# A hybrid decoder block: Toeplitz transfers issued by POOL, and two groups of loads kept in program order

## The chip, the cores and the metric

The kernel runs on one core of one Trainium2 chip. A core has five engines, each with its own queue of instructions that it works off in order: PE (TensorE, matmuls), DVE (VectorE), ACT (ScalarE), POOL (GpSimd) and SP (SyncE, which here only issues DMA transfers). A transfer is issued by an engine's queue and then moved by 16 DMA engines that all queues share. Transfers issued by SP appear in the profile under the hardware queue, those issued by POOL under the software queue. The metric is the device time of one execution, in microseconds (us); lower is better. The time before is the median of three runs, 1581.86 us (1578.76 to 1582.31).

## The reference

One decoder block over 1024 tokens and 16 meta tokens, model width 1024, float32. Two mixers run on one projection of the layer-normed input, their gated sum is projected and added, and a feed-forward layer follows:

```
p     = h @ w_in + b_in          # u_s5 | q | k | v | o | i | f | g_s5 | g_m
y_s5  = z[..., :D] * sigmoid(z[..., D:]),  z = gelu(S5(u_s5)) @ s5_w_glu
y_m   = (sigmoid(o) * HeadNorm(mLSTM(silu(conv(q,k)), v, i, f))) @ m_w_out
mix   = sigmoid(g_s5) * y_s5 + sigmoid(g_m) * y_m
h     = LN(alpha * h + mix @ w_o)
h     = LN(alpha * h + relu(h @ w_up + b_up)^2 @ w_down)
```

S5 is a linear state-space recurrence: 32 groups of 16 channels, each with 64 complex states, `x_t = Abar x_{t-1} + Bbar u_t`, `y_t = Re(C x_t) + D u_t`.

## The kernel before

Activations are kept with the feature on the partition. Each float32 product is made of three matmuls in a reduced format (lines 226 to 228): both operands are split into a high and a low part (`whi`, `wlo` for weights; `hT_hi`, `hT_lo` for activations), with ACT copying the high part and DVE subtracting it for the low one. Weights come in as `wraw`, by line 198 for plain jobs and by line 1024 for the stage described below.

The projection runs as a list of jobs (q, k, v, o, u, g for each tile of columns), and smaller work is woven between the jobs' matmuls: lanes of generators are advanced as estimated PE time passes, each `yield` naming how long to wait until the next piece. The S5 mixer, the mLSTM's chunks and the preparation of later weights are such lanes. The order that is written this way is only a draft: a scheduler (line 2074) reorders the instructions of every engine by its own estimate of durations, within the data dependencies. Instructions wrapped in `tc.keep_in_program_order` keep the order in which they were written among themselves.

**S5.** The 32 groups go through in four blocks b = 0 to 3 of eight groups. The 1024 + 16 positions are cut into 130 columns of 8 steps. `s5_consts(b)` makes the matrices of a block: `s5Mi` (input to state), `s5RS` (state to output), `s5Kt` (the convolution kernel of the 8 steps, 32 partitions) and from it `s5Mx`, the lower-triangular Toeplitz matrix. POOL clears `s5Mx` (line 753), and sixteen small transfers (line 758: 8 shifts x 2 halves, 16 partitions x 4 x 128 down to 16 elements, 32 KB down to 4 KB) lay `s5Kt` out along its diagonals; 64 of them in all. Then POOL writes the first two columns of the rotation table `s5T` (lines 764 to 767), and DVE doubles it seven times (lines 572 to 577).

`u_load(b)` brings the block's input back from memory, regrouped, as `s5U` in eight transfers (line 786). `s5_batch(b)` multiplies it into states on PE (`s5z`, line 802; ACT and DVE move the result out, lines 810 and 812), scans them on DVE (lines 817 to 846, tables `s5T`, result `s5w`) and makes the output on PE (`s5y`: line 857 with `s5Mx` and `s5U`, line 858 with `s5RS` and `s5w`). It is stored to `ys_dr` (line 863), read back regrouped in eight transfers `s5yc` (line 871), and after the GELU split into `gelh` and `gell` (lines 877 and 878) for the GLU jobs z0 to z7.

**Then** come the GLU jobs, and a stage called `Seven`, a seven-product scheme in place of eight for the last gates (`g`) and for `m_w_out` (`y`). It needs sums of weights, which POOL makes by accumulating transfers during the projection (`ws_dr`, line 974, each behind a small copy `mark`, line 972, that waits for a job's weights), activations as `rawb` (line 991, eight transfers of 512 KB) with sums on DVE (line 1002) and splits (lines 997 and 998), and its weights by line 1024 into a ring of three buffers, split at lines 1042 and 1043.

**Beside it** run two lanes whose transfers share SP's queue: `ah_scale` (loads `ahr` 1377, DVE 1386, stores `ah_dr` 1388) and `up_early` (loads `wur` 1404, sums on DVE, stores `wu_dr` 1414), which prepares weight sums for the feed-forward layer. The tiles named here live in one pool of 30 slots of 4 KB per partition, so a load can also wait until the last reader of its slot is done.

Of the kernel before, what the change touches and what calls it, by code (L numbers as in the profile page):

```python
# [14 lines left out]
P = 128  # L15
# [97 lines left out]
def decoder_block(  # L113
# [4 lines left out]
    nc = tc.nc  # L118
    v_, a_, g_, t_ = nc.vector, nc.scalar, nc.gpsimd, nc.tensor
# [9 lines left out]
    def slot(name, dt=F32):  # L129
        return big.tile([P, SLOT], dt, tag="s", name=name)  # L130
# [404 lines left out]
    def u_job(i):  # L535
        st = {}

        def evac(bi, c0, c1, ps):
            if bi == 0:
                st["u"] = slot("uT")  # L540
            o = st["u"][:, :LEN].rearrange("p (j c) -> p c j", j=8)
            a_.activation(o[:, c0 // 8:c1 // 8, :], ps.rearrange("p (c j) -> p c j", j=8), AF.Identity,
                          bias=bft[:, JU + i:JU + i + 1])

        def done():
            nc.sync.dma_start(us_dr[i * P:(i + 1) * P].rearrange("p j c -> p (j c)"), st["u"][:, :LEN])
            UD.add(i)
            lanes["s5c"].add(s5_consts(i))
            lanes["s5"].add(s5_batch(i))
        fm_job(JU + i, BLK, 0, evac, done)  # L550
# [123 lines left out]
    def s5_consts(b):  # L674
# [49 lines left out]
        for ri in range(2):  # L724
            for g2 in range(2):
                s = slice(64 * g2, 64 * g2 + 64)
# [27 lines left out]
        mx = Mx[:, 0:1024].rearrange("p (q g t) -> p q g t", q=4, g=2)  # L754
        kt = Kt.rearrange("p (q t) -> p q t", q=4)
        for j in range(8):
            for g2 in range(2):
                nc.sync.dma_start(mx[16 * j:16 * j + 16, :, g2, 16 * j:P],
                                  kt[16 * g2:16 * g2 + 16, :, 0:P - 16 * j])
        yield K5[b]  # L760
        T = slot("s5T")
        tc_, ts_ = (T[:, i * 520:(i + 1) * 520].rearrange("p (q c) -> p q c", q=4) for i in range(2))
# [220 lines left out]
    def s3(t):  # L983
        return t[:, :1024].rearrange("p (k s) -> p k s", k=2)

    def raw_block(dr, kh, ch, off=0):
        ts = [slot("rawb"), slot("rawb")]
        for i in range(2):
            k = 4 * kh + 2 * i
            c = off + 512 * ch  # L990
            nc.sync.dma_start(s3(ts[i]), dr[k:k + 2, :, c:c + 512].rearrange("k p s -> p k s"))
        return ts

    def to_home(ts, hm):
# [9 lines left out]
    class Seven:  # L1004
# [8 lines left out]
        def load(self, i):  # L1013
            if i >= self.ntile():
                return
            r = ring[0].tile([P, 1024], F32, tag="wr", bufs=3, name="wraw")
            for j, (n, p) in enumerate(self.units[2 * i:2 * i + 2]):
                s = {5: 0, 6: 1, 7: 2, 3: 3}.get(n)
                if s is None:
                    t = self.w[self.i0 + 2 * p + (n == 4)].rearrange("p k f -> p (k f)")  # L1020
                    a = t[:, 0:512] if n == 1 else t[:, 512:1024]
                else:
                    a = ws_dr[self.p0 + p, s]
                nc.sync.dma_start(r[:, j * 512:j * 512 + 512], a)
            self.raw[i] = r

        def split(self, i):
# [115 lines left out]
    def gates_and_output():  # L1143
# [5 lines left out]
        def begin():  # L1149
            for nm, kh, ch in (("12", 0, 1), ("22", 1, 1), ("11", 0, 0), ("21", 1, 0)):  # L1150
                R[nm] = raw_block(h_dr, kh, ch, META)
# [12 lines left out]
        def hm_load():  # L1164
            for nm, kh, ch in (("11", 0, 0), ("12", 0, 1), ("22", 1, 1), ("21", 1, 0)):
                M[nm] = raw_block(hm_dr, kh, ch)
# [250 lines left out]
    for w in ORDER.split():  # L1417
        n, i = w[0], int(w[1:])
# [22 lines left out]
    for w in LOAD0.split():  # L1441
        i = int(w[1])
# [635 lines left out]
```

## Time and profile before

| what | value |
| --- | --- |
| runs | 1581.86 us median (1578.76 to 1582.31) |
| profiled execution | 1577.87 us, span from first to last instruction 1576.1 us |
| mean granted TensorE clock | 0.984 |
| PE busy | 1516.2 us, 96% |
| DVE, ACT, POOL busy | 1079.4, 642.8 and 70.2 us (68, 41 and 4%) |
| line 758 on SP | 64 transfers, median 593 ns each |
| hardware queue, software queue | 234.18 MB and 25.82 MB |

A busy share is an average over the whole span; a stage is read from a table of stages. In a row of a timeline stand the start, the duration, engine, line, operation, output and input, a count (xN: as many in a row), and in brackets the idle time just before with what ended it. A row of waits reads: engine, tile and line that waited, what it waited for, total us, number of times, longest. An engine with a q (SPq) stands for its queue, where issuing and waiting for a transfer is shown. In rows of a line's transfers the three durations are minimum, median and maximum in ns.

### The profile page before, as it was taken

The page shows a single profiled execution, that of the slowest core. Times are in us where ns is not written, and L with a number is a line of the kernel's source. Part 1 is how long each engine was busy: PE and PEld are TensorE (multiplying, and loading weights), DVE is VectorE, ACT ScalarE, POOL GpSimd, SP SyncE. Part 2 cuts the span into 40 slices and gives each one's busy share as a digit, 9 for nine tenths or more (in the row PEclk, how much of TensorE's full clock was granted, in tenths as well). Part 3 has the DMA queues.
Part 4 walks back from the last instruction along what each step waited for, and adds up shares of the span by engine and source line. Part 5 has one row for each costly group of instructions (what it writes and reads, how often), then busy time and mean ns, then how long its engine had stood idle before and what let it go on. Part 6 is the DMA issues. An engine that isn't in the chain of part 4 may idle for free.

```text
span 1576.1 us, 20513 instructions
## 1 busy us (share of the span) xinstructions
PE 1516.2 (96%) x7593; PEld 1278.9 (81%) x7593; DVE 1079.4 (68%) x2083; ACT 642.8 (41%) x982; POOL 70.2 (4%) x131
## 2 busy tenths in 40 slices
PE   8999999998899798999999999999999999999997
PEld 8998998997777686777788888888888888888886
DVE  7666555678667455568879575666666779776776
ACT  6523444335254333235635234444444534433340
POOL 0000011111001010000000001000000000000000
PEclk9999999999999899999999999999999999999999
DMA  8412324414344466685344317744443799667642
GB/s 310 157 56 63 97 61 133 119 31 121 108 115 99 151 181 217 226 317 200 102 149 144 108 54 242 246 145 149 147 147 134 220 366 335 220 227 239 222 166 107
DMA packets 140580, 261.31 MB, mean 166 GB/s; under 512 B 34224, under 2 KB 56184, under 8 KB 140424
## 3 DMA queue, kind: packets, MB, share of 16 engines
q1 hardware_dynamic: 116464, 234.18, 43.8%
q0 software_dynamic: 24016, 25.82, 6.7%
q8 instruction: 59, 0.97, 0.2%
q14 instruction: 41, 0.34, 0.1%
HBM read 188.78 MB, written 84.55 MB: 173 GB/s over the span
## 4 chain that ended last, share of the span: by engine, by line
PE 39%; issue 15%; DMA 2%; DVE 1%; ACT 0%; SPq 0%; POOLq 0%; DVEq 0%; ACTq 0%
PE mm L228 10%; PE mm L227 9%; PE mm L226 9%; PE sd L227 3%; PE sd L226 3%; PE sd L228 3%; DMA wur<-in_wup_dram 1%; DMA wu_dr<-wpre 1%; DMA rawb<-h_dr 1%; PE ln L1565 0%; DVE rawb L1002 0%; DVE wpre L1413 0%; DVE sgs L945 0%; DVE z2s L944 0%; DVE wlo L1043 0%
## 5 line engine op out<-in xcount | busy, mean ns | idle before, releaser
L226 PE MATMUL mm<-hT_hi,whi 128*128 128x512 f32 (+3 forms) x604 | 229.0, 379 | 1.4 <-ACT whi L212 1.4
L228 PE MATMUL mm<-hT_hi,wlo 128*128 128x512 f32 (+3 forms) x604 | 224.7, 377 | 3.9 <-DVE wlo L1043 3.9
L227 PE MATMUL mm<-hT_lo,whi 128*128 128x512 f32 (+3 forms) x604 | 227.5, 377 | 0.0
L228 PEld LDWEIGHTS mm<-hT_hi,wlo 128*128 128x128 f32 x604 | 113.7, 188 | 22.5 <-DVE wlo L1043 5.2
L226 PEld LDWEIGHTS mm<-hT_hi,whi 128*128 128x128 f32 x604 | 114.2, 189 | 19.6 <-ACT whi L212 1.8
L227 PEld LDWEIGHTS mm<-hT_lo,whi 128*128 128x128 f32 x604 | 114.1, 189 | 17.7 <-issue 0.4
L227 PE MATMUL sd<-dwl,dah 128*128 128x512 f32 x240 | 94.4, 393 | 0.0
L228 PE MATMUL sd<-dwh,dal 128*128 128x512 f32 x240 | 94.1, 393 | 0.0
L1777 ACT ACTIVATE dwh<-wdr 128x1024 fp32r<-128x1024 f32 x56 | 59.0, 1054 | 86.2 <-DMA wdr<-in_wdn_dram 28.1
L226 PE MATMUL sd<-dwh,dah 128*128 128x512 f32 x240 | 94.1, 393 | 0.0
L1773 ACT ACTIVATE dah<-da 128x1024 fp32r<-128x1024 f32 x56 | 58.7, 1051 | 84.8 <-PE sd L227 37.8
L1774 DVE TENSOR_TENSOR dal<-da,dah 128x1024 fp32r<-128x1024 f32 x56 | 68.2, 1220 | 24.1 <-ACT dah L1773 23.5
L227 PE MATMUL mm<-dwl,dah 128*128 128x512 f32 (+1 forms) x224 | 84.5, 378 | 0.0
L228 PE MATMUL mm<-dwh,dal 128*128 128x512 f32 (+1 forms) x224 | 84.4, 377 | 0.0
L226 PE MATMUL mm<-dwh,dah 128*128 128x512 f32 (+1 forms) x224 | 84.2, 377 | 0.0
L1778 DVE TENSOR_TENSOR dwl<-wdr,dwh 128x1024 fp32r<-128x1024 f32 x56 | 68.2, 1220 | 12.4 <-ACT dwh L1777 11.8
L226 PE MATMUL mm<-whi,hT_hi 128*128 128x256 f32 (+1 forms) x256 | 75.3, 294 | 0.0
L228 PE MATMUL mm<-whi,hT_lo 128*128 128x256 f32 (+1 forms) x256 | 74.6, 291 | 0.0
L227 PE MATMUL mm<-wlo,hT_hi 128*128 128x256 f32 (+1 forms) x256 | 73.9, 289 | 0.0
L213 DVE TENSOR_TENSOR wlo<-wraw,whi 128x1024 fp32r<-128x1024 f32 (+1 forms) x46 | 56.1, 1223 | 18.0 <-ACT whi L212 15.2
L228 PE MATMUL mm<-th,wul 128*128 128x512 f32 x156 | 61.6, 395 | 0.0
L227 PE MATMUL mm<-tl,wuh 128*128 128x512 f32 x156 | 61.5, 394 | 0.0
(473 smaller groups left out, 3679.8 us busy)
## 6 DMA issues: line engine op xcount, KB each, us to landing
da<-act_dr SPq DMA_DIRECT2D x56, 512.0 KB, 5.5
wdr<-in_wdn_dram SPq DMA_DIRECT2D x56, 512.0 KB, 6.2
wur<-in_wup_dram SPq DMA_DIRECT2D x32, 512.0 KB, 4.4
act_dr<-upy SPq DMA_DIRECT2D x64, 256.0 KB, 2.5
wraw<-in_wf_dram SPq DMA_DIRECT2D x30, 512.0 KB, 6.7
wu_dr<-wpre SPq DMA_DIRECT2D x21, 512.0 KB, 4.5
wpre<-wu_dr POOLq DMA_DIRECT2D x21, 512.0 KB, 5.3
act_dr<-upx SPq DMA_DIRECT2D x32, 256.0 KB, 3.0
```

Source lines behind the costliest of these rows:

```text
L213: todo.append(lambda e=v_, r=r, hi=hi, lo=lo, n=n: e.tensor_tensor(lo[:, :n], r[:, :n], f32(hi[:, :n]), op=OP.subtract))
L226: t_.matmul(ps, ah, bh, start=(i == 0 and part[0]), stop=False, skip_group_check=skip)
L227: t_.matmul(ps, ah, bl, start=False, stop=False, skip_group_check=skip)
L228: t_.matmul(ps, al, bh, start=False, stop=(i == n - 1 and part[1]), skip_group_check=skip)
L1773: a_.activation(ah[:, :D], a[:, :D], AF.Copy)
L1774: v_.tensor_tensor(alo[:, :D], a[:, :D], f32(ah[:, :D]), op=OP.subtract)
L1777: a_.activation(wh, raw[i], AF.Copy)
L1778: v_.tensor_tensor(wl, raw[i], f32(wh), op=OP.subtract)
```

## The change

Three edits. The sixteen transfers of each `s5Mx` go from SP's queue to POOL's. The loads of `rawb` (line 991) and the weight loads of `Seven` (line 1024) are wrapped so that they keep the order in which the program writes them.

```diff
@@ s5_consts
-                nc.sync.dma_start(mx[16 * j:16 * j + 16, :, g2, 16 * j:P],
-                                  kt[16 * g2:16 * g2 + 16, :, 0:P - 16 * j])
+                g_.dma_start(mx[16 * j:16 * j + 16, :, g2, 16 * j:P],
+                              kt[16 * g2:16 * g2 + 16, :, 0:P - 16 * j])
@@ raw_block
-            nc.sync.dma_start(s3(ts[i]), dr[k:k + 2, :, c:c + 512].rearrange("k p s -> p k s"))
+            tc.keep_in_program_order(nc.sync.dma_start(s3(ts[i]), dr[k:k + 2, :, c:c + 512].rearrange("k p s -> p k s")))
@@ Seven.load
-                nc.sync.dma_start(r[:, j * 512:j * 512 + 512], a)
+                tc.keep_in_program_order(nc.sync.dma_start(r[:, j * 512:j * 512 + 512], a))
```

Since the scheduler orders each engine, the three edits move instructions elsewhere too; the differences run from the constants of block 0 to the output projection. On SP, at the loads of block 1's input, this is the difference (minus: the row stood here before; plus: it stands here now; x7: seven in a row; the last numbers are the shape):

```order
-L786 DMA s5U<-us_dr 16x8x130 x7
-L758 DMA s5Mx<-s5Kt 16x4x128 x2
...
-L758 DMA s5Mx<-s5Kt 16x4x16 x2
-L786 DMA s5U<-us_dr 16x8x130
+L546 DMA us_dr<-uT 128x1040
+L198 DMA wraw<-in_wf_dram 128x1024
+L786 DMA s5U<-us_dr 16x8x130 x8
 L198 DMA wraw<-in_wf_dram 128x1024
```

The sixteen Toeplitz transfers that stood between the seventh and the eighth load are gone, and the eight loads stand together. The same holds for block 3, where three loads stood ahead of the transfers and five behind them. On POOL, at block 0, the transfers are put ahead of the first columns of the rotation table:

```order
 L753 MEMSET s5Mx 128x1024
+L758 DMA s5Mx<-s5Kt 16x4x128 x2
+L758 DMA s5Mx<-s5Kt 16x4x112 x2
+L758 DMA s5Mx<-s5Kt 16x4x96 x2
+L758 DMA s5Mx<-s5Kt 16x4x80 x2
+L758 DMA s5Mx<-s5Kt 16x4x64 x2
+L758 DMA s5Mx<-s5Kt 16x4x48 x2
+L758 DMA s5Mx<-s5Kt 16x4x32 x2
+L758 DMA s5Mx<-s5Kt 16x4x16 x2
 L764 MEMSET s5T 128x4
```

In blocks 1 to 3 they stand behind these columns (lines 764 to 767) and ahead of the next `mark` and `ws_dr`. The third place is on SP ahead of the gate products of `Seven`; the six loads of `in_wf` are those of its first three weight tiles:

```order
 L1372 DMA bB_5618<-in_ln0r_dram 128x1024
 L1377 DMA ahr<-ah_dr 128x1024
-L1024 DMA wraw<-in_wf_dram 128x512 x6
 L1388 DMA ah_dr<-ahr 128x1024
...
 L991 DMA rawb<-h_dr 128x2x512 x8
+L1024 DMA wraw<-in_wf_dram 128x512 x6
 L1024 DMA wraw<-ws_dr 128x512 x6
```

They stood behind the first load of `ah_scale` and now stand behind the eight `rawb` loads. On DVE the low part of the first of these tiles (line 1043) moves behind the first three sums of line 1002 and the next ones, to where the second tile's stood; on ACT its high part (line 1042) moves behind the first `hT_hi` of line 997. On PE the `s5z` matmuls of blocks 1 and 3 are spread over more places, and block 0's `s5y` with `s5w` (line 858) stands some 36 matmuls later.

## The prediction

> **What bounds the kernel now.** I read the page's engine shares first, then the stage table, then what PE (TensorE) waits for, then the timelines round the waits that the change can touch.
>
> ```profile
> PE 1516.2 (96%) x7593; PEld 1278.9 (81%) x7593; DVE 1079.4 (68%) x2083; ACT 642.8 (41%) x982; POOL 70.2 (4%) x131
> ...
> 360.00:400.00 40.00, 28.70 (x167) 26.03 (x166) 28.99 (x91) 18.28 (x27) 7.09 (x7) 0.85 0.42 120
> ...
> 520.00:560.00 40.00, 30.44 (x133) 24.98 (x132) 20.07 (x53) 8.46 (x16) 3.00 (x3) 0.87 0.49 149
> ...
> 720.00:1576.00 856.00, 847.12 (x3734) 689.33 (x3732) 614.83 (x897) 353.62 (x529) 12.36 (x22) 1.00 0.55 186
> ```
>
> The first row says that PE bounds the kernel: 1516.2 of a 1576.1 us span, so 60 us of idle time are all that reordering can win. The stage rows (length, then busy us of PE, PEld, DVE, ACT, POOL, the granted clock, DMA share, GB/s) say where they lie: 11.3 us between 360 and 400 and 9.6 us between 520 and 560, with a granted clock of 0.85 and 0.87 in just these stages. Behind 720 PE idles 9 us in 856, and there the change reorders only a few loads.
>
> ```profile
> PE s5z L802 <- DMA s5U<-us_dr: 15.3, 2, 9.6
> PE mm L227 <- DVE gell L878: 7.0, 1, 7.0
> PE s5y L858 <- DVE s5w L846: 6.0, 3, 4.3
> PE mm L228 <- DVE wlo L1043: 3.9, 2, 2.8
> ```
>
> These are PE's four largest waits (total us, times, longest). All four lie inside the region that the change reorders; the first is the loads of S5 input that stand on SP's queue among the Toeplitz transfers:
>
> ```profile
> 368.62 6.73 SPq L786 DMA_DIRECT2D s5U<-us_dr  x7
> 378.24 11.42 SPq L758 DMA_DIRECT2D s5Mx<-s5Kt  x16
> 389.70 0.58 SPq L786 DMA_DIRECT2D s5U<-us_dr  x1
> ...
> 500.68 1.27 SPq L786 DMA_DIRECT2D s5U<-us_dr  x3
> 514.88 10.82 SPq L758 DMA_DIRECT2D s5Mx<-s5Kt  x16
> 532.71 2.20 SPq L786 DMA_DIRECT2D s5U<-us_dr  x5
> ```
>
> Seven of block 1's eight pieces go out by 375.4; the eighth stands behind sixteen Mx transfers and leaves at 389.70. In block 3 five of eight stand behind them and leave at 532.71. PE answers:
>
> ```profile
> 398.38 2.07 PE L802 MATMUL s5z<-s5U,s5Mi 128*128 128x130 f32 x8 [5.73 <-DMA s5U<-us_dr]
> ...
> 400.32 0.78 PE L226 MATMUL mm<-hT_hi,whi 128*128 128x512 f32 x1
> ...
> 401.64 0.39 PE L227 MATMUL mm<-hT_lo,whi 128*128 128x512 f32 x1
> 401.87 0.40 PE L228 MATMUL mm<-hT_hi,wlo 128*128 128x512 f32 x1
> ...
> 537.46 2.94 PE L802 MATMUL s5z<-s5U,s5Mi 128*128 128x130 f32 x12 [9.56 <-DMA s5U<-us_dr]
> ```
>
> **The change, part by part.**
>
> *The eighth and the last five pieces leave early.* With the Mx transfers on POOL, the eight loads stand together on SP. Block 1's eighth would leave by about 375.8; even at the slowest landing of that line (8.7 us, the next fence) it is there at 384.5, and PE stood idle only from 392.65. That removes 5.73 us and the slow restart behind it: three steps from 400.32 to 401.64 took 1.32 us where the steady pace (401.64 to 401.87) makes it 0.69, so 0.6 us more. **A = -6.4 us.** In block 3 the five leave with the first three near 501–504 and are there by about 512, against an idle PE from 527.9: 9.56 + 0.6, **B = -10.2 us.** Both rest on no other wait taking the place.
>
> ```profile
> DMA to landing us min/median/max: 2.3/3.8/8.7
> ...
> L758 SPq DMA_DIRECT2D s5Mx<-s5Kt x64: 585/593/1835, 329.5 to 525.1; - x64
> ...
> L1621 POOL DMA_DIRECT2D wpre<-wu_dr x21: 527/528/616, 834.4 to 992.0; - x21
> ...
> L974 POOL DMA_DIRECT2D ws_dr<-in_wmo_dram x6: 1117/1354/1942, 267.8 to 620.3; - x6
> ...
> L766 POOL COPY s5T<-s_p x4: 189/480/5255, 325.1 to 502.8; 128x4 f32<-128x4 f32 x4
> ```
>
> *What POOL pays.* No Mx transfer was ever issued on POOL, so its price is bounded: below by POOL's loads of 128x1024 (0.53 us), above by its largest weight sum (1.94 us). An Mx piece is small and plain, so I take 0.6 us: 16 x 0.6 = 9.6 us for a block, 38 us in all on an engine that is busy for 4%. For blocks 1 to 3 the issues stand behind the block's T copies and ahead of the next ws_dr sum; what waits is the s5y matmul. Block 3's last piece went out at 525.7 on SP, and the first matmul that reads it stood at 557.9 (about 539 with A to C): 12 us to spare at least, and block 0, the one without spare time, is next.
>
> ```profile
> L857 PE MATMUL s5y<-s5U,s5Mx x16: 271/275/275, 557.9 to 573.7; 128*128 128x128 f32 x16
> ...
> 329.45 10.89 SPq L758 DMA_DIRECT2D s5Mx<-s5Kt  x16
> ...
> 325.01 0.10 POOL L764 MEMSET s5T<- 128x4 f32 x1 [11.39 <-PE s5p L733]
> ...
> 331.25 0.16 DVE L572 TENSOR_TENSOR s5tt<-s5T 128x4 f32<-128x4 f32 x1
> ...
> 349.24 0.15 DVE L577 TENSOR_TENSOR s5T<-s5tt 128x4 f32<-128x4 f32 x1
> ...
> 359.84 0.70 DVE L817 TENSOR_TENSOR s5w<-s5Z,s5T 128x520 f32<-128x520 f32 x1
> ```
>
> *Block 0.* POOL's T start (325.01) now stands behind the sixteen issues, which can begin only at 329.45: 329.45 + 9.6 = 339, and the DVE doublings, which took 331.25 to 349.4 mixed with other work, end at 357 if they take the same 18 us. Their reader L817 stood at 359.84, so the cover is 3 us. PE's L858 that waited 4.3 us here is now placed about 36 matmuls (36 x 0.23 = 8.3 us) later. So the stall becomes 4.3 - 8.3 + d for a chain late by d: gone at d = 0 (-4.3), +8 at d = 16. I take **C = -2 us.**
>
> ```profile
> 546.09 0.38 SPq L1377 DMA_DIRECT2D ahr<-ah_dr  x1
> 558.47 3.56 SPq L1024 DMA_DIRECT2D wraw<-in_wf_dram  x6
> ...
> 580.72 0.38 SPq L863 DMA_DIRECT2D ys_dr<-s5Y  x1
> ...
> 616.30 0.79 PE L227 MATMUL mm<-gell,whi 128*128 128x512 f32 x1 [7.04 <-DVE gell L878]
> ```
>
> *The six weight loads of L1024 leave this place.* They held SP from 546.5 to 562.0, and the ahr loads, the last ys_dr store and its reads stood behind them; PE's wait for the last gell at 616.30 ends that chain. It can lose all 7.0 us or nothing, as ahr work still precedes gell on DVE: **D = -4 us.**
>
> *Where they go.* They now stand behind the eight rawb loads, and the first whi/wlo of the gate run go where the second tile's stood:
>
> ```profile
> 694.10 5.93 SPq L991 DMA_DIRECT2D rawb<-h_dr  x8
> ...
> 707.42 1.22 DVE L1043 TENSOR_TENSOR wlo<-wraw,whi 128x1024 fp32r<-128x1024 f32 x1
> ...
> 716.04 1.22 DVE L1043 TENSOR_TENSOR wlo<-wraw,whi 128x1024 fp32r<-128x1024 f32 x1
> ...
> 717.31 0.50 PE L228 MATMUL mm<-hT_hi,wlo 128*128 128x512 f32 x1 [2.79 <-DVE wlo L1043]
> ```
>
> Tile 0 is then ready at 717.3, not 708.6; PE has 24 matmuls of it to do (24 x 0.23 = 5.6 us) before it reaches the second tile, where it stood at 717.31 before. That is +5.6; +10 if the loads also land late (last issue at 700.0 + 3.6, landing up to 16.1 as at 558, then 2.3 us of splitting), 0 if the rawb loads come ahead by as much. **E = +6 us.**
>
> Sum: -6.4 - 10.2 - 2 - 4 + 6 = **-16.6 us.** The profiled execution took 1577.87 us (span 1576.1 and 1.8 around it), so 1561.3; the median of the runs shown, 1581.86, is 4.0 above the profiled one, so **1565 us** by the runs.
>
> *A rule against it.* The row to weigh is L766: a 128x4 copy on POOL took 5.26 us at 367.33 while DVE was in back-to-back two-input work, and 0.19 at its best. The Trainium skill (DMA: Bandwidth & Descriptors, section SWDGE vs HWDGE vs iDMA) says why POOL is the wrong home for small plain transfers: there the descriptors are written by POOL into SBUF, which DVE can lock it out of, while transfers issued from SP are immune. Its page SBUF — State Buffer (section SBUF: two separate sides) gives some 3.1 us for such a transfer beside a DVE copy where it takes 0.62 alone; by that estimate a block's sixteen issues take 50 us and the time is that of the rival *starved POOL* at its far end, about 1600 us. The row agrees that POOL can be held up; that an issue is held up no row of before shows beyond 1.94 us.
>
> **The rivals.**
>
> *Starved POOL (slower).* At 1.94 us an issue, block 0's sixteen take 31 us, to 360.5; with a 5.3 us copy and 18 us of doublings L817 starts at 384, d = 24, and the stall at L858 is 4.3 - 8.3 + 24 = 20, so C = +16 in place of -2: sum +1.4, 1583 by the runs. From 2.2 us an issue it is slower by over 0.2%; at three microseconds blocks 1 and 3 wait too. For: L766. Against: L1621's 21 issues all within 0.53 to 0.62, on a chip whose DVE is busy for 68%.
>
> ```profile
> 630.53 0.81 SPq L1404 DMA_DIRECT2D wur<-in_wup_dram  x2
> ...
> 686.83 7.22 SPq L1414 DMA_DIRECT2D wu_dr<-wpre  x7
> ```
>
> *The gain stops at 630 (same).* The early up-projection sums run on SP from the first wur loads (630.53) to the last wu_dr stores, and the rawb loads (694.10) stand right behind them. If these are paced by something that does not come ahead, the gate run begins when it did, and A to D are given back there, with E left: between -4 and +6, about 1583 by the runs. For: nothing in the change speeds that chain up. Against: on SP it stands behind the ahr loads and stores, which B and D bring forward.
>
> *Half of it (faster, less).* The stall of block 3 passes to DVE's chain (s5Z to L846) at the next s5y matmul, where only 2 us were waited before: B = -3, D = 0: sum -5.4, 1576.
> **How the numbers follow.** The forecast (1554 to 1573) has 0.50, half of it 0.17, the gain stopping 0.13, starved POOL 0.20. A measurement of this kernel tells some 0.2%, 3.2 us, from no change: faster 0.65 (the forecast and most of the half), same 0.14, slower 0.21 (starved POOL and an unlucky E). The forecast with its best ends (C -4.3, D -7.0, E 0) is -28, 1554; its worst (C +8, D 0, E +10) is +1.4, 1583. The range 1553 to 1584 takes in the middle rivals and leaves out the far end of starved POOL.
>
> **What would show it.** Right: s5U x8 in one row of SP's timeline for blocks 1 and 3, no PE wait on s5U, the clock of 360–400 and 520–560 near 1.00, L758 on POOL at 0.5 to 0.7 us, an L858 stall of block 0 under 5 us, and a new PE wait of 5 to 11 us on L1043 or L1042 at the start of the gate run. Wrong: L758 on POOL above 1.5 us, PE waiting on s5w or s5Mx in block 0, or the rawb loads still issued near 694.

## The result, and the profile after

The changed kernel takes 1565.08 us (median of 1562.89 to 1567.97) against 1581.4 us for the kernel before on the same chip; the ratio is 0.9914 with a 95% interval of 0.9896 to 0.9933, a gain of 13.6 us (10.6 to 16.4); the two medians lie 16.3 us apart. The forecast was 1565, faster, and its range 1553 to 1584. The profiled execution took 1566.04 us, 11.8 less than the one before, with a span of 1564.2 in place of 1576.1.

PE's busy time is what it was, and the time went out of its waits. The mean granted clock of the profiled execution is 0.984 before and after: the new stalls have slow stretches of their own. The page's shares and PE's largest waits after the change:

```profile
PE 1515.8 (97%) x7593; PEld 1278.7 (82%) x7593; DVE 1079.9 (69%) x2083; ACT 642.7 (41%) x982; POOL 102.2 (7%) x195
```

```profile
PE mm L226 <- ACT whi L1042: 5.4, 1, 5.4
PE mm L228 <- DVE wlo L213: 4.9, 4, 3.7
...
PE mm L227 <- DVE gell L878: 3.1, 1, 3.1
...
PE s5k L741 <- DVE s5Ri L719: 2.9, 1, 2.9
PE mm L226 <- DVE z2s L944: 2.1, 1, 2.1
...
PE mm L228 <- DVE wlo L1043: 1.9, 1, 1.9
...
PE s5y L858 <- DVE s5w L846: 1.2, 1, 1.2
```

The 15.3 us of waiting for `s5U` are gone from the list; the wait for `gell` fell from 7.0 to 3.1, those for `s5w` from 6.0 to 1.2. New are 5.4 us on L1042 at the start of the gate run, 2.9 on `s5Ri`, and 3.7 on a `wlo` of line 213. On SP the loads of blocks 1 and 3 now stand together, each block's in one row, and on POOL the sixteen issues of block 0 take 8.1 us:

```profile
372.95 3.64 SPq L786 DMA_DIRECT2D s5U<-us_dr  x8
...
498.77 3.64 SPq L786 DMA_DIRECT2D s5U<-us_dr  x8
...
529.75 0.33 SPq L1377 DMA_DIRECT2D ahr<-ah_dr  x1
552.71 0.33 SPq L1388 DMA_DIRECT2D ah_dr<-ahr  x1
...
566.56 0.32 SPq L863 DMA_DIRECT2D ys_dr<-s5Y  x1
...
676.63 6.08 SPq L991 DMA_DIRECT2D rawb<-h_dr  x8
682.75 6.99 SPq L1024 DMA_DIRECT2D wraw<-in_wf_dram  x6
```

```profile
329.94 8.14 POOL L758 DMA_DIRECT2D s5Mx<-s5Kt  x16 [16.38 <-DVE s5Kt L745]
338.07 0.12 POOL L764 MEMSET s5T<- 128x4 f32 x1
...
373.94 6.26 POOL L766 COPY s5T<-s_p 128x4 f32<-128x4 f32 x1
380.15 3.06 POOL L767 COPY s5T<-s_p 128x4 f32<-128x4 f32 x1
383.14 4.06 POOL L758 DMA_DIRECT2D s5Mx<-s5Kt  x8
```

By stages, the one round block 3's stall is now full, while the one round block 0 and the start of block 1 still idles 7.7 us (11.3 before), and 320 to 360 idles 1.7 us where it had no idle time:

```profile
320.00:360.00 40.00, 38.32 (x265) 36.16 (x265) 23.69 (x77) 12.34 (x28) 10.61 (x27) 1.00 0.19 51
360.00:400.00 40.00, 32.31 (x179) 28.61 (x178) 37.92 (x129) 18.74 (x30) 19.07 (x23) 0.83 0.40 109
...
520.00:560.00 40.00, 40.00 (x197) 33.33 (x197) 26.93 (x58) 16.20 (x23) 7.75 (x13) 1.00 0.59 173
```

### The profile page after: what moved, and what is told of

Its sections match the earlier page's. It is cut to its first block, busy times and chain, and to the rows that moved or that the text cites. A ratio compares the mean times of both kernels' runs of the same rounds, so it can differ in the third digit from the quotient of the medians.

```text
span 1564.2 us, 20543 instructions
## 1 busy us (share of the span) xinstructions
PE 1515.8 (97%) x7593; PEld 1278.7 (82%) x7593; DVE 1079.9 (69%) x2083; ACT 642.7 (41%) x982; POOL 102.2 (7%) x195
## 4 chain that ended last, share of the span: by engine, by line
PE 31%; issue 23%; DMA 3%; DVE 2%; ACT 0%; SPq 0%; POOL 0%; POOLq 0%; DVEq 0%
PE mm L228 7%; PE mm L227 7%; PE mm L226 7%; PE sd L227 3%; PE sd L226 3%; PE sd L228 3%; DMA wpre<-wu_dr 1%; DMA rawb<-h_dr 1%; DMA wu_dr<-wpre 1%; DMA wur<-in_wup_dram 0%; DVE wlo L1043 0%; DVE wlo L213 0%; DMA woraw<-in_wo_dram 0%; POOL wpre L1621 0%; SPq L991 0%
## 5 line engine op out<-in xcount | busy, mean ns | idle before, releaser
L226 PE MATMUL mm<-hT_hi,whi 128*128 128x512 f32 (+3 forms) x604 | 231.0, 382 | 8.0 <-ACT whi L1042 5.4
L226 PEld LDWEIGHTS mm<-hT_hi,whi 128*128 128x128 f32 x604 | 115.7, 192 | 26.6 <-ACT whi L1042 6.2
L226 PE MATMUL sd<-dwh,dah 128*128 128x512 f32 x240 | 94.2, 393 | 0.0
L226 PE MATMUL mm<-dwh,dah 128*128 128x512 f32 (+1 forms) x224 | 84.4, 377 | 0.0
L226 PE MATMUL mm<-whi,hT_hi 128*128 128x256 f32 (+1 forms) x256 | 75.2, 294 | 0.0
```

The lines of the kernel that those rows point to most:

```text
L226: t_.matmul(ps, ah, bh, start=(i == 0 and part[0]), stop=False, skip_group_check=skip)
```

## The experiments

Nine kernels, each timed in five rounds beside the kernel before (1579 to 1580 us in these rounds); the ratios are to that kernel, with 95% intervals.

### e1 and e2: the two halves of the change

e1 is the kernel before with the first edit alone, e2 with the other two alone:

```diff
e1  -                nc.sync.dma_start(mx[16 * j:16 * j + 16, :, g2, 16 * j:P],
    +                g_.dma_start(mx[16 * j:16 * j + 16, :, g2, 16 * j:P],
e2  -            nc.sync.dma_start(s3(ts[i]), ...)
    +            tc.keep_in_program_order(nc.sync.dma_start(s3(ts[i]), ...))
    -                nc.sync.dma_start(r[:, j * 512:j * 512 + 512], a)
    +                tc.keep_in_program_order(nc.sync.dma_start(r[:, j * 512:j * 512 + 512], a))
```

> Only the 64 Mx transfers go to POOL; the loads of lines 991 and 1024 are left to the scheduler as before, so the six weight loads stand again behind the first ahr load and hold SP there. Theory (the gain is that of the S5 loads, and the order of the weight loads is worth about nothing: 2.4 us less waiting for gell, 3.4 us more at the gate run): 1564 us, between 1561 and 1567, no PE wait on s5U, the gate run's stall back at about 4 us, the gell stall at about 6. Rival (SP's freedom from the weight loads carries a good part of the gain): 1570 or more, with ahr, ys_dr and gell late by 5 us and more.

> Only the loads of lines 991 and 1024 are kept in program order; the Mx transfers stay on SP. Theory: 1582 us, between 1579 and 1585: PE still waits 5.7 and 9.6 us for s5U, the gell stall is smaller by 2 us, the gate run's larger by 3. Rival (the program order brings part of the gain): 1577 or less.

Measured: e1 1566.9 us, ratio 0.9909 (0.9893 to 0.9926); e2 1580.8 us, ratio 1.0001 (0.9989 to 1.0014). The whole gain is the first edit's. The program order alone is worth nothing that can be measured, and the waits show why: it exchanges a shorter wait for `gell` (3.0 in place of 7.0) for a longer one at the gate run (5.5 and 1.9 in place of 1.1 and 2.8). In e1 the weight loads stand behind the first ahr load again, and PE's waits are the other way round:

```profile
PE mm L227 <- DVE gell L878: 6.0, 1, 6.0
PE mm L228 <- DVE wlo L213: 5.3, 4, 4.0
...
PE mm L228 <- DVE wlo L1043: 3.2, 2, 2.8
PE s5k L741 <- DVE s5Ri L719: 2.9, 1, 2.9
```

The rival that SP's freedom from the weight loads carries the gain falls. In the rows of SP's order shown above only line 1024's loads change place; the two groups of loads were not wrapped one at a time.

### e6 and e7: block 3 alone and block 1 alone

```diff
-                nc.sync.dma_start(mx[16 * j:16 * j + 16, :, g2, 16 * j:P],
+                (g_ if b == 3 else nc.sync).dma_start(mx[16 * j:16 * j + 16, :, g2, 16 * j:P],
```

(e7: `b == 1`.)

> The kernel before, with the sixteen Mx transfers of block 3 alone on POOL. Theory: the stall of 9.6 us and its restart go, nothing else: 1570 us, between 1567 and 1573. Rival (the stall passes on to another wait of block 3's chain or is given back before the GLU jobs): 1575 or more.

> The kernel before, with the sixteen Mx transfers of block 1 alone on POOL. Theory: the stall of 5.7 us and its restart go: 1574 us, between 1571 and 1577; the 4.3 us wait on s5w in block 0 stays, since the rotation table of block 0 keeps its place. Rival (the stall passes to the next wait): 1578 or more.

Measured: e6 1569.2 us, ratio 0.9930 (0.9909 to 0.9951), 11.1 us less; e7 1569.9 us, ratio 0.9938 (0.9917 to 0.9958), 9.8 us less, which is more than theory allowed. Each run loses its one stall and keeps the other (6.0 us on `s5U` at 397.5 in e6, 9.6 at 528.5 in e7). So neither stall passes on whole to a later wait: e7 has no new one, and in e6 a wait of 2.6 us on `gelh` (line 877) is new, while that on `gell` is 1.2 us shorter. What the waits leave unexplained in both is about 2 us of slow PE behind each stall: from L226 at 371.22 to L463 at 461.96, before, PE takes 90.7 us, in e7 82.6 for the same 406 matmuls, while the stalls between the two shrank by 6.1; for e6 the same reckoning, from the `s5y` wait at 513 to the one on `gell` (401 matmuls in both), gives 10.0 against 8.1. The clock shows it. Before the change, by short stretches (the last row lies in block 3's stall):

```profile
392.00:396.00 4.00, 0.65 (x4) 0.31 (x2) 0.98 (x2) 0.97 (x1) 0.00 (x0) 0.83 0.11 49
396.00:400.00 4.00, 1.62 (x7) 1.65 (x8) 0.07 (x1) 0.27 (x1) 0.00 (x0) 0.50 0.57 142
400.00:404.00 4.00, 4.00 (x18) 3.30 (x17) 2.91 (x7) 2.08 (x5) 0.00 (x0) 0.81 0.71 281
...
532.00:536.00 4.00, 0.00 (x0) 0.00 (x0) 0.00 (x0) 0.00 (x0) 0.00 (x0) 0.50 0.37 87
```

and in e7:

```profile
392.00:396.00 4.00, 4.00 (x21) 3.34 (x20) 3.45 (x12) 2.48 (x5) 0.00 (x0) 1.00 0.38 158
396.00:400.00 4.00, 4.00 (x24) 3.48 (x23) 3.68 (x12) 1.02 (x4) 0.00 (x0) 1.00 0.51 177
```

In both stalls the granted clock falls to 0.50, and the eight `s5z` matmuls that end block 1's run at that clock too: they took 2.07 us and start 0.22 us apart. Four at full clock took 0.61 (the row below); less the 0.28 of the last one, that is 0.11 apart. That is 0.9 us which the forecast missed, beside the 0.6 that it read from the next matmuls; what makes up the rest of the 2 us was not separated. The Trainium skill (TensorE: Matmul & The Clock Gate, section What's actually happening) has this as a gate that passes half the pulses after an idle window of some 3.4 us and all of them only after as long a busy one; the rows agree with the half, and with a stall of 5.7 us being long enough.

```profile
357.12 0.61 PE L802 MATMUL s5z<-s5U,s5Mi 128*128 128x130 f32 x4
```

### e3 and e9: what block 0 lost

Together e6 and e7 won 20.9 us, yet e1, which does both and blocks 0 and 2 besides, won 14.4. The missing 6.5 us (5 either way, by the three intervals) were looked for in block 0. e3 writes POOL's first columns of the rotation table ahead of Mx; e9 puts block 0's transfers alone back on SP:

```diff
e3           yield C5[b]
    +        T = slot("s5T")
    +        ...
    +        g_.tensor_copy(ts_[:, :, 1], S5["p8"][:, 1, q0:q0 + 4])
             Mx = slot("s5Mx")
             g_.memset(Mx[:, 0:1024], 0.0)
             ...
             yield K5[b]
    -        T = slot("s5T")
    -        ...
    -        g_.tensor_copy(ts_[:, :, 1], S5["p8"][:, 1, q0:q0 + 4])
e9  -                g_.dma_start(mx[16 * j:16 * j + 16, :, g2, 16 * j:P],
    +                (g_ if b else nc.sync).dma_start(mx[16 * j:16 * j + 16, :, g2, 16 * j:P],
```

> The changed kernel, with POOL's first columns of the rotation table written in the program ahead of the clearing of Mx and of its transfers, so that the doublings on DVE do not stand behind them. Theory (block 0's chain came 10 us late, L817 at 369.5 in place of 359.8, because of the order in which the doublings were put, not because of what POOL or DVE is slowed by): L817 back near 360, the PE waits on s5k, wlo and v in 345 to 390 fall from 9 us to under 5, time 1560 us, between 1558 and 1562. Rival (the transfers on POOL slow DVE or come late by themselves): L817 stays near 369 or the doublings take as long as their delay, 1564 to 1567.

> The changed kernel with block 0's sixteen Mx transfers alone back on SP; blocks 1 to 3 stay on POOL, the loads stay in program order. Theory (6 to 7 us of the expected gain were lost in block 0, because the rotation table's first columns stood behind the transfers on POOL): L817 of block 0 back near 360, no PE wait on s5k or on a wlo between 370 and 385, the old 4.4 us wait on s5w back in its place: 1559 us, between 1557 and 1562. Rival (the loss lies in the later blocks, whose own Mx is later on POOL, and the mend with the columns first won its 9 us there): 1564 to 1567.

Measured: e3 1555.7 us, ratio 0.9842 (0.9824 to 0.9861); e9 1557.4 us, ratio 0.9870 (0.9847 to 0.9894), 20.5 us less than before, within half a microsecond the sum of e6 and e7. So the loss is block 0's. (e3 came out 2.3 us below the range expected of it, as e4 did below by 1.1: that the waits took their slow restarts along would explain it, but was not separated.) How it came about stands on DVE. Of the changed kernel:

```profile
341.77 0.16 DVE L492 TENSOR_SCALAR dd<-pn 128x1 f32<-128x1 f32 x1 [2.96 <-PE pn L474]
...
346.62 0.16 DVE L572 TENSOR_TENSOR s5tt<-s5T 128x4 f32<-128x4 f32 x1
...
369.53 0.69 DVE L817 TENSOR_TENSOR s5w<-s5Z,s5T 128x520 f32<-128x520 f32 x1
372.17 0.75 DVE L719 SCALAR_TENSOR_TENSOR s5Ri<-s5tm 128x576 f32<-128x576 f32 x1
...
381.93 1.21 DVE L213 TENSOR_TENSOR wlo<-wraw,whi 128x1024 fp32r<-128x1024 f32 x1
```

and of e3:

```profile
361.10 0.70 DVE L817 TENSOR_TENSOR s5w<-s5Z,s5T 128x520 f32<-128x520 f32 x1
364.84 0.75 DVE L719 SCALAR_TENSOR_TENSOR s5Ri<-s5tm 128x576 f32<-128x576 f32 x1
371.85 2.79 DVE L846 TENSOR_TENSOR s5w<-s5Z,s5w 64x512 f32<-64x512 f32 x4
```

In the changed kernel POOL had the columns ready at 338.5, but the first doubling ran at 346.62: the scheduler had put the mLSTM's small steps ahead of the doublings on DVE, and these wait for PE and ACT, one after another. DVE was busy for 23.7 us between 320 and 360 (30.8 before), was then behind by 10 us, and PE waited not for the S5 chain but for what stood behind it on DVE: `s5Ri` at 372.97 (2.9 us) and a weight's low half at 383.19 (3.7 us). With the columns first (e3), or with the transfers back on SP (e9, L817 at 358.01), both waits are gone; in e9 block 0's old wait on `s5w` is back at 3.0 us, where 4.4 were expected. Two things delay the doublings: the columns are ready some 13 us later than before (338.5 against 325.4), and DVE has another order. e3 and e9 take away both at once, so the share of each is not shown. POOL's transfers as such did not slow DVE: in e3 they take as long and stand in the same stretch (331.23, 8.13 us).

### e4 and e5: the gate run's start, and both mends

```diff
e4           for nm, kh, ch in (("12", 0, 1), ("22", 1, 1), ("11", 0, 0), ("21", 1, 0)):
    +            if nm == "11":
    +                [g.load(i) for i in range(3)]
                 R[nm] = raw_block(h_dr, kh, ch, META)
         def first():
    -        for i in range(3):
    -            g.load(i)
```

Both start from the changed kernel; e5 is e3 and e4 together.

> The changed kernel, with the three first weight tiles of the gate run loaded after four of the eight rawb loads instead of after all eight. Theory (the 7.3 us stall at the start of the gate run comes from the place of these loads): stall of 3 us or less, 1561 us, between 1559 and 1563. Rival (the run waits for the rawb data and the sums on DVE however the weights stand): the stall passes to the second or third tile, 1564 to 1567.

> The changed kernel with both mends: the rotation table's first columns ahead of Mx on POOL, and the three first weight tiles of the gate run after four of the eight rawb loads. If the two losses are separate, as theory has it, their gains add: 1565 - 9 - 6 = 1550 us, between 1547 and 1553. Rival (both take the same time out of the same chain, so that the second finds nothing left): 1555 to 1558.

Measured: e4 1557.9 us, ratio 0.9852 (0.9835 to 0.9870); e5 1548.7 us, ratio 0.9803 (0.9779 to 0.9828), 31 us less than before and the fastest here. The mends add: by the medians e3 takes 9.4 us off the changed kernel, e4 7.2, and both 16.3. PE at the start of the gate run, of the changed kernel and of e4:

```profile
694.65 0.79 PE L226 MATMUL mm<-hT_hi,whi 128*128 128x512 f32 x1 [5.39 <-ACT whi L1042]
698.63 0.79 PE L228 MATMUL mm<-hT_hi,wlo 128*128 128x512 f32 x1 [1.91 <-DVE wlo L1043]
```

```profile
697.14 0.50 PE L228 MATMUL mm<-hT_hi,wlo 128*128 128x512 f32 x1 [1.89 <-DVE wlo L1043]
703.95 0.50 PE L228 MATMUL mm<-hT_hi,wlo 128*128 128x512 f32 x1 [0.90 <-DVE wlo L1043]
```

The waits shrink by 4.5 us, and the first matmul behind them takes 0.50 us, not 0.79: between 692 and 700 the changed kernel's clock was 0.50. The medians differ by 7.2 us, the gains over the kernel before by 9.8; what of the rest is the clock and what the scatter of the runs was not separated.

### e8: the transfers on ACT

```diff
-                nc.sync.dma_start(mx[16 * j:16 * j + 16, :, g2, 16 * j:P],
+                a_.dma_start(mx[16 * j:16 * j + 16, :, g2, 16 * j:P],
```

> The kernel before, with all 64 Mx transfers issued by ACT in place of SP (a hardware queue, but an engine that is busy for 41%). Theory (any queue but SP's frees the s5U loads, yet ACT's own instructions behind the sixteen issues come about 9 us late, and PE waits for its whi and s5Z copies): the s5U stalls go, new PE waits on ACT of 3 to 10 us: 1570 us, between 1564 and 1577. Rival (where the transfers are issued does not matter once they are off SP): 1566 or less.

Measured: 1590.5 us, ratio 1.0074 (1.0051 to 1.0097): slower than before, against both readings. The `s5U` waits are gone here too, but ACT's next instructions stand behind the issues, and PE waits for them:

```profile
328.55 8.73 ACTq L758 DMA_DIRECT2D s5Mx<-s5Kt  x13
337.33 1.26 ACT L514 ACTIVATE hmF<-pt,mngt 128x512 f32<-128x512 f32 x2 [8.26 <-DMA s5Mx<-s5Kt]
...
382.14 9.00 ACTq L758 DMA_DIRECT2D s5Mx<-s5Kt  x14
391.24 0.60 ACT L861 ACTIVATE s5Y<-s5y 128x512 f32<-128x512 f32 x1 [9.89 <-DMA wraw<-in_wf_dram]
```

Of what waited for these transfers on ACT, `hraw` of line 496 waited longest, behind block 2's sixteen issues (443.87 to 462.78), and PE's largest wait at 463.4 is for it:

```profile
  ACT hraw L496: 18.5, 1
```

PE's waits in e8:

```profile
PE pu L477 <- ACT hraw L496: 8.2, 1, 8.2
PE mm L228 <- DVE wlo L213: 7.2, 8, 2.6
...
PE pk L458 <- ACT s5Kt L742: 4.2, 1, 4.2
```

To take the transfers off SP was not enough; they needed a queue on which little is awaited.

## Why the prediction was right, and where it was not

The time came out as forecast and the main mechanism too, but a hit to within 0.1 us is luck. The gain that was forecast, 16.6 us, lies just above the 10.6 to 16.4 that were measured, and terms of the sum were off in both directions. One of the signs named for being right did not come: the clock between 360 and 400 stayed at 0.83, where block 0's new stalls fall.

**A and B (-6.4 and -10.2): right, with one part too small.** e7 and e6 give -9.8 (3 either way) and -11.1 (3 either way), so the forecast of A lies just outside e7's interval and that of B well inside e6's; by the traces the two stretches are 8.2 and 10.0 us shorter. The part that was mis-sized in both is the slow restart: 0.6 us was read from the large matmuls, while the `s5z` matmuls ahead of them already ran at half the clock; about 2 us each by the traces. In block 3 the new wait on `gelh` took about as much back.

**C (-2): wrong in sign.** By e1 against e6 and e7, and by e9 (6.9 us less than the changed kernel), block 0 cost about 6.5 us. What failed is the sentence that the doublings "end at 357 if they take the same 18 us", begun when POOL is done: they began 8 us after POOL was done, as DVE's new order had other work ahead of them that waits for PE and ACT, took 22 us, and ended at 369. The forecast put such a lag at nothing, though its own rows of before show one: POOL's columns from 325.01, the first doubling at 331.25. L817 came 9.7 us late. That PE's L858 had been moved out of the way held (block 0's wait of 4.3 us on `s5w` is gone); that others were queued behind the late chain on DVE (`s5Ri`, a `wlo`) was not looked for, and it was they that PE waited for.

**D and E (-4 and +6, together +2): right as a sum, within the noise.** e2 measures 0.2 us more (1.7 less to 2.2 more). On the profiles D is -3.9 for the wait on `gell`, of which 1.5 came back as a longer wait on z2s, and E is +3.4 in waits, more with the clock behind them. E's mechanism, tile 0 where the second tile's stood, is confirmed by e4.

**The price of POOL (0.6 us an issue): right.** 64 issues took 512 ns each, 567 at most:

```profile
L758 POOL DMA_DIRECT2D s5Mx<-s5Kt x64: 512/512/567, 329.9 to 524.2; - x64
...
DMA to landing us min/median/max: 1.6/3.0/17.4
```

So *starved POOL* is out: no issue was held up, with DVE busy for 37.9 of 40 us beside block 1's. The same stretch holds POOL's 128x4 copies up for 6.26 and 3.06 us: here it was copies that were held, not issues. The Trainium skill's 3.1 us (SBUF — State Buffer, section SBUF: two separate sides) are for a transfer beside a DVE `tensor_copy`, and the same section says that `tensor_tensor` did not stall transfers. The runs agree with the second, as the DVE work beside the issues was nearly all of two inputs (`TENSOR_TENSOR` and the like); the first is not put to the test here. The 17.4 us landing is block 2's, behind a weight sum on the same queue; it has time there.

*The gain stops at 630* is out: wur, wu_dr and the rawb loads came ahead with the rest (rawb at 676.6, 17.5 us earlier). *Half of it* is out by e6.

## What to carry to other kernels

Count what a queue makes wait, not only what it issues: a few late pieces behind a burst of small transfers cost PE 15 us of waiting and some 4 us of half-speed matmuls behind it. Here the burst did best on a queue where little else is awaited, and whatever a third engine needs from that queue is to be written ahead of the burst. Where a scheduler orders the engines, look at the new order of every engine whose inputs are said to come later: the loss of block 0 stood in what was put ahead of the doublings, and behind them, on DVE, and in columns written behind the burst, not in any transfer's duration.

## What was not expected of the hardware

The restart after a PE stall cost more than the 0.6 us that were forecast: in stalls of 5.7 us and 9.6 us the clock fell to 0.50, and the slow matmuls behind them cost about 2 us each. A transfer issued by POOL was no dearer than on SP (512 ns against 593) or on ACT (606), though POOL's own small copies were held for up to 6.3 us in the same stretch.
